# Tokens first, small constants on a second queue, the second block's rows loaded in that block, and dummy products during the load, in a two-block fp32 transformer on one core

## The chip, the cores and the metric

The kernel runs on one NeuronCore of a Trainium2 chip, as one launch. The time is the device time of that core in microseconds (us). The engines in what follows are TensorE (PE, with its weight loads shown apart as PEld), VectorE (DVE), ScalarE (ACT), GpSimd (POOL) and SyncE (SP), which here only issues DMAs. Each engine takes its instructions in a fixed order and waits at semaphores for what another engine or a DMA has not delivered yet.

## The reference, cut to what matters

Two model blocks run one after the other on 256 tokens of width 1024, each with two layers, all in fp32. The part that the change is near is the beginning of each block.

```python
# first block, layer i
u = rmsnorm(h, norm_mix[i])
proj = u @ w_in[i]                                   # gz, ga and gb are among its columns
g = -jnp.exp(a_log) * jax.nn.softplus(ga + dt_bias)  # 8 heads
...
# second block, layer l
u = rms_norm(h, norm1_g[l])
proj = u @ w_in[l]
log_a = log_sigmoid(g_lr @ w_gate2 + b_gate) / 16    # gated linear attention
lam = exp(sum(lq1 * lk1)) - exp(sum(lq2 * lk2)) + lambda_init   # differential attention
```

Between those stand the mixers, a dense and a mixture-of-experts feed-forward part, gated per-layer embeddings, the residual sums and the norms.

## The kernel before

The tokens `h` lie in SBUF as 128 partitions x 2 token halves x 1024. Every large product is done to near fp32 precision out of three reduced-precision products: a weight block `raw` (up to 512 KB) comes by DMA, ACT rounds it into `whi` (line 247), DVE takes the rest into `wlo` (line 248), and PE adds `whi x uh`, `wlo x uh` and `whi x ul` in PSUM (lines 195 to 197, and 221 to 223 for products that come out transposed). `uh` and `ul` are the same two parts of the normed, transposed activations: PE transposes 128x128 pieces of `h` with the identity `ident` (line 263), ACT scales by the norm's weights in `cols` and rounds (line 250), DVE takes the rest (line 251). The norm's factor R comes from squares on ACT (line 281, `junk`) and a Newton iteration on DVE (lines 144 to 152), and is applied after the product.

Weights pass through six `raw` buffers and three pairs of `whi`/`wlo`, so a load waits for the DVE instruction that last read its buffer, and a rounding waits for the PE instruction that last read its pair. SP issues all of the loads.

The order on each engine is set by a scheduler that places instructions by a model of their durations and by priorities. `high_priority(offset=100000)` puts the first loads of `run` ahead of everything. Weight loads have a high priority too, constants have none. A change in the first instructions therefore moves others further on.

`run` begins with the identity, the first half of the tokens' columns, `cols` (161 KB: all norm weights and the convolution's weights of both blocks), the second half of the tokens, and `rows` (400 KB: 800 numbers, read 128 times so that every partition has them). `rows` holds `a_log` and `dt_bias` of the first block (used at line 381, `nea`, and line 376, `xa`) and, for the second block, the four vectors behind `lam` (line 1170, `lt`) and the gate's bias (line 1078, `la`). In the second block the first projections are `grg` and `gla`; 16 columns of `grg` are copied (`glr`, line 1067), transposed on PE (line 1070), copied (`glt`, line 1072) and multiplied by a small weight (line 1076), and `la` adds the bias to that. The next projection, `dq`, runs on PE around these.

Of the kernel before, what the change touches and what calls it, by code (L numbers as in the profile page):

```python
# [9 lines left out]
F32 = mybir.dt.float32  # L10
F32R = mybir.dt.float32r
# [10 lines left out]
RAW2 = 6  # L22
CONV = 800
CRIT = 50
DQ = lambda nc: [nc.scalar]
ORDER = "z v0 v1 v2 v3 rg i0 d0+i1 d1 rq rk rv".split()
D = 1024
# [11 lines left out]
def _consts():  # L39
# [29 lines left out]
    for g, w in enumerate((2, 4, 8, 16)):  # L69
# [16 lines left out]

COLS1 = (("norm_mix", 8), ("norm_ffn", 8), ("norm_ple", 8), ("ret_gn", 8), ("gdn_gn", 1), ("conv_w", 96))
COLS2 = (("norm1_g_2", 8), ("pool_scale_2", 2), ("diff_norm_g_2", 4), ("gla_norm_g_2", 2), ("norm2_g_2", 8), ("norm_final", 8))
ROWS = (("a_log", 8), ("dt_bias", 8), ("diff_lq1_2", 64), ("diff_lk1_2", 64), ("diff_lq2_2", 64),
        ("diff_lk2_2", 64), ("gla_b_gate_2", 128))  # L90


def _offsets(spec):
    o, out = 0, {}
    for l in range(2):
        for n, w in spec:
            out[n, l] = (o, w)
            o += w
    return out, o


COL_AT, NCOL = _offsets(COLS1 + COLS2)
ROW_AT, NROW = _offsets(ROWS)


class Net:
# [27 lines left out]
        return s.cols[:, o:o + w]  # L134

    def row(s, name, l):
        o, w = ROW_AT[name, l]
        return s.rows[:, o:o + w]

    def rsqrt(s, ss, n, mul, add):  # L140

# [1145 lines left out]
    def run(s, out, stop=None):  # L1287
        nc, a = s.nc, s.a
        h = s.hp.tile([P, 2, D], F32, name="h")
        hv = lambda ap: ap.rearrange("(t p) d -> p t d", p=P)  # L1290
        s.cols = s.const.tile([P, NCOL], F32, name="cols")
        with s.tc.high_priority(offset=100000):
            s.ident = s.cst("ident", s.const)
            for c in (0, 512):
                nc.sync.dma_start(h[:, :, c:c + 512], hv(a["x"])[:, :, c:c + 512])
                if c == 0:
                    nc.sync.dma_start(s.cols, a["cols"])
        s.rows = s.const.tile([P, NROW], F32, name="rows")
        src = a["rows"]
        with s.tc.high_priority(offset=100000):  # L1300
            nc.sync.dma_start(s.rows, bass.AP(tensor=src.tensor, offset=src.offset, ap=[[0, P], [1, NROW]]))

        def done(tag):
            if stop == tag:
                nc.sync.dma_start(hv(out), h)
                return True
            return False
        with ExitStack() as es:
            for l in range(2):
                with ExitStack() as e2:  # L1310
                    cp = e2.enter_context(s.tc.tile_pool(name="cp1", bufs=1))
                    s.c = {n: s.cst(n, cp) for n in C1[1:]}
                    s.mixer1(h, l)
                if done(f"mix{l}"):
                    return
                with ExitStack() as e2:
                    yp = e2.enter_context(s.tc.tile_pool(name="yp", bufs=1))
                    y = yp.tile([P, 2, D], F32, name="y")
                    if l == 0:
                        with ExitStack() as e3:  # L1320
                            pp = e3.enter_context(s.tc.tile_pool(name="py", bufs=1))
                            room = [[pp.tile([P, 2, n], F32R, name=f"py{n}{i}") for i in range(2)] for n in (D, T)]
                            run = s.ple_y(y, l, room)
                            u, R = s.norm_t(h, s.col("norm_ffn", l))
                            run()
                        s.swiglu(h, u, R, a["ffn_w_gate"], a["ffn_w_up"], a["ffn_w_down"], 2816)
                        ahead = ()
                    else:
                        pre = yp.tile([P, 2048], F32, name="pre")
                        nc.sync.dma_start(pre.rearrange("p (k c) -> p k c", k=4),  # L1330
                                          a["w_ple_gate"][l][:512, :512].rearrange("(k p) c -> p k c", p=P))
                        ahead = ((0, 2, pre[:, :1024]), (2, 2, pre[:, 1024:]))
                        s.raws.append(e2.enter_context(s.tc.tile_pool(name="raw2", bufs=RAW2)))
                        s.moe(h, l, y)
                    if done(f"ffn{l}"):
                        return
                    s.ple(h, l, y, ahead)
                    s.raws = s.raws[:1]
                if done(f"ple{l}"):
                    return  # L1340
            ur = s.norm_between(h)
        if done("first"):
            return
        with ExitStack() as es:
            cp = es.enter_context(s.tc.tile_pool(name="cp2", bufs=1))
            s.c = {n: s.cst(n, cp) for n in C2}
            s.kz = []
            for i in range(4):
                kz = cp.tile([P, 2, T], F32, name=f"kz{i}")
                nc.gpsimd.memset(kz, 0.0)  # L1350
                s.kz.append(kz)
            for l in range(2):
                s.mixer2(h, l, ur if l == 0 else s.norm_t(h, s.col("norm1_g_2", l)))
                if done(f"mix2{l}"):
                    return
                s.mlp2(h, l)
                if done(f"mlp2{l}"):
                    return
            s.final(h, out, "final_norm_g_2", cp)


def _arrays(inp):

    n = {k: np.asarray(v) for k, v in inp.items()}
    out = {"x": n["x"].reshape(T, D), "pT": n["p"].reshape(2, T, 256).transpose(0, 2, 1)}
    for k in ("w_in", "w_br_ret", "w_br_gdn", "w_out", "w_ple", "w_ple_gate", "w_in_2", "w_out_2", "w_mlp1_2",
              "w_mlp2_2", "pool_w_2", "gla_w_gate2_2", "norm_final", "final_norm_g_2"):
        out[k] = n[k]
    for k in ("ffn_w_gate", "ffn_w_up", "ffn_w_down", "router", "exp_w_gate", "exp_w_up", "exp_w_down"):
        out[k] = n[k][0]  # L1370

    for k in ("w_mlp1_2", "ffn_w_gate", "ffn_w_up"):
        w = out[k].reshape(-1, 8, P, out[k].shape[-1] // P, P).transpose(0, 3, 2, 1, 4)
        out[k] = w.reshape((2,) * (k == "w_mlp1_2") + (-1, P, D))
    cols, rows = [], []
    for l in range(2):
        for k, w in COLS1 + COLS2:
            v = n[k] if k == "norm_final" else n[k][l]
            if k == "conv_w":
                cols.append(v.reshape(4, 24, P).transpose(2, 1, 0).reshape(P, 96))  # L1380
            else:
                cols.append(v.reshape(w, P).T)
        for k, w in ROWS:
            rows.append(n[k][l])
    out["cols"] = np.concatenate(cols, 1)
    out["rows"] = np.concatenate(rows)
    for k, v in _consts().items():
        out["c_" + k] = v
    return {k: np.ascontiguousarray(v) for k, v in out.items()}
# [23 lines left out]
```

## Time and profile before

| | |
|---|---|
| median of 3 runs | 1980.87 us (1978.38 to 1981.93) |
| the profiled execution | 1982.7 us, span of its instructions 1980.8 us |
| PE busy | 1935.2 us, 98% of the span |
| DVE, ACT busy | 1461.8 us (74%), 1187.4 us (60%) |
| mean granted TensorE clock | 0.994 of full speed |
| bytes moved by DMA | 395.47 MB, mean 200 GB/s |

The span is cut by the page into 40 slices, and PE is busy for eight tenths of the first and nine tenths or more of most others. So what any stage is worth is the idle time of PE in it, and whether PE ran at full or at half clock there. Times in rows are counted from the start of the span.

### The profile page before, as it was taken

To read this page: it belongs to the slowest core of one execution; us is meant where nothing else is said; L and a number is where in the kernel's file an instruction comes from. 1 tells how busy PE (TensorE), PEld (TensorE's weight loads), DVE (VectorE), ACT (ScalarE), POOL (GpSimd) and SP (SyncE) were. 2 spreads that over 40 slices of the span, in tenths; PEclk is the share of its full clock that TensorE was granted. 3 is DMA by queue.
4 is the path that set the end of the run, shared out by engine and by line. 5 is a ranking of instruction groups with operands and counts; after the bars stand their busy time and mean duration, and the time that the engine had idled before them with its cause. 6 is when DMAs were issued, how large, how long until landed. Compare 5 with 4: busy or idle time off the path is not lost. (4 is left out here: it accounts for less than half of the span.)

```text
span 1980.8 us, 30212 instructions
## 1 busy us (share of the span) xinstructions
PE 1935.2 (98%) x11194; PEld 1646.6 (83%) x11194; DVE 1461.8 (74%) x2623; ACT 1187.4 (60%) x1889; POOL 13.7 (1%) x29
## 2 busy tenths in 40 slices
PE   8999999999999999999999999998999999999998
PEld 7887787999889877777888888786879898879896
DVE  7987676656479895767998988897877565777565
ACT  7864445544478753446877777776765454565453
POOL 0000000000000000001000000000000000000000
PEclk9999999999999999999999999999999999999999
DMA  8556335555565564356798989994735555525552
GB/s 244 151 172 190 102 134 177 174 184 188 184 184 151 164 187 133 120 192 213 270 347 302 354 297 356 325 353 150 227 107 161 191 190 173 182 97 180 191 182 106
DMA packets 252699, 395.47 MB, mean 200 GB/s; under 512 B 31328, under 2 KB 107264, under 8 KB 252544
## 3 DMA queue, kind: packets, MB, share of 16 engines
q1 hardware_dynamic: 235056, 389.27, 59.9%
q10 hardware_dynamic: 17488, 4.20, 1.1%
q8 instruction: 90, 1.47, 0.3%
q14 instruction: 65, 0.53, 0.1%
HBM read 390.79 MB, written 2.62 MB: 199 GB/s over the span
## 5 line engine op out<-in xcount | busy, mean ns | idle before, releaser
L248 DVE TENSOR_TENSOR wlo<-raw,whi 128x1024 fp32r<-128x1024 f32 (+3 forms) x748 | 878.6, 1184 | 359.3 <-ACT whi L247 349.2
L247 ACT ACTIVATE whi<-raw 128x1024 fp32r<-128x1024 f32 (+3 forms) x748 | 765.5, 1027 | 609.4 <-PE mm L197 362.6
L195 PE MATMUL mm<-whi,uh 128*128 128x512 f32 (+3 forms) x1312 | 505.4, 386 | 4.8 <-ACT mgg L640 2.2
L196 PE MATMUL mm<-wlo,uh 128*128 128x512 f32 (+3 forms) x1312 | 506.9, 387 | 2.3 <-DVE wlo L248 1.9
L197 PE MATMUL mm<-whi,ul 128*128 128x512 f32 (+3 forms) x1312 | 505.7, 387 | 0.3
L196 PEld LDWEIGHTS mm<-wlo,uh 128*128 128x128 f32 x1312 | 248.3, 189 | 55.5 <-DVE wlo L248 9.7
L195 PEld LDWEIGHTS mm<-whi,uh 128*128 128x128 f32 x1312 | 248.0, 189 | 52.4 <-ACT uh L250 3.2
L197 PEld LDWEIGHTS mm<-whi,ul 128*128 128x128 f32 x1312 | 247.8, 189 | 45.9 <-DVE ul L251 1.6
L239 PE MATMUL mm<-uh,whi 128*128 128x256 f32 x864 | 242.6, 281 | 0.8 <-ACT uh L250 0.6
L241 PE MATMUL mm<-uh,wlo 128*128 128x256 f32 x864 | 242.4, 281 | 0.0
L240 PE MATMUL mm<-ul,whi 128*128 128x256 f32 x864 | 242.3, 281 | 0.0
L239 PEld LDWEIGHTS mm<-uh,whi 128*128 128x128 f32 x864 | 162.9, 189 | 1.9 <-ACT uh L250 1.1
L240 PEld LDWEIGHTS mm<-ul,whi 128*128 128x128 f32 x864 | 162.9, 188 | 0.2
L241 PEld LDWEIGHTS mm<-uh,wlo 128*128 128x128 f32 x864 | 162.9, 189 | 0.0
L197 PE MATMUL mm<-whi,hl 128*128 128x512 f32 x344 | 136.4, 397 | 0.0
L196 PE MATMUL mm<-wlo,hh 128*128 128x512 f32 x344 | 135.7, 394 | 0.0
L195 PE MATMUL mm<-whi,hh 128*128 128x512 f32 x344 | 134.5, 391 | 0.0
L223 PE MATMUL mm<-uh,wlo 128*128 128x256 f32 x384 | 109.8, 286 | 0.0
L221 PE MATMUL mm<-uh,whi 128*128 128x256 f32 x384 | 109.6, 285 | 0.0
L222 PE MATMUL mm<-ul,whi 128*128 128x256 f32 x384 | 109.5, 285 | 0.0
L196 PEld LDWEIGHTS mm<-wlo,hh 128*128 128x128 f32 x344 | 64.6, 188 | 15.2
L250 ACT ACTIVATE uh<-pt,cols 128x256 fp32r<-128x256 f32 x152 | 65.0, 472 | 19.6 <-PE pt L263 7.2
(409 smaller groups left out, 2383.6 us busy)
## 6 DMA issues: line engine op xcount, KB each, us to landing
raw<-in_w_in_dram SPq DMA_DIRECT2D x176, 512.0 KB, 3.6
raw<-in_w_mlp_dram SPq DMA_DIRECT2D x128, 512.0 KB, 3.6
raw<-in_exp_w_down_dram SPq DMA_DIRECT2D x80, 512.0 KB, 5.9
raw<-in_exp_w_gate_dram SPq DMA_DIRECT2D x64, 512.0 KB, 5.2
raw<-in_exp_w_up_dram SPq DMA_DIRECT2D x64, 512.0 KB, 5.7
raw<-in_w_out_dram SPq DMA_DIRECT2D x32, 512.0 KB, 3.6
raw<-in_exp_w_gate_dram SPq DMA_DIRECT2D x32, 384.0 KB, 4.4
raw<-in_exp_w_up_dram SPq DMA_DIRECT2D x32, 384.0 KB, 4.0
```

Source lines behind the costliest of these rows:

```text
L195: nc.tensor.matmul(o, uh[:, u0 + k, tk], hi, start=first and k == 0, stop=False)
L196: nc.tensor.matmul(o, uh[:, u0 + k, tk], lo, start=False, stop=False)
L197: nc.tensor.matmul(o, ul[:, u0 + k, tk], hi, start=False, stop=last and k == kt - 1)
L221: nc.tensor.matmul(o[:, m], hi[:, k], uh[:, k, :], start=k == 0, stop=False)
L222: nc.tensor.matmul(o[:, m], hi[:, k], ul[:, k, :], start=False, stop=False)
L223: nc.tensor.matmul(o[:, m], lo[:, k], uh[:, k, :], start=False, stop=k == 7)
L239: nc.tensor.matmul(o[:, i], hi[:, k], uh[:, k, :], start=k == 0, stop=False)
L240: nc.tensor.matmul(o[:, i], hi[:, k], ul[:, k, :], start=False, stop=False)
L241: nc.tensor.matmul(o[:, i], lo[:, k], uh[:, k, :], start=False, stop=k == 7)
L247: nc.scalar.activation(hi, src, AF.Copy)
L248: nc.vector.tensor_sub(lo, src, hi.bitcast(F32))
L250: nc.scalar.activation(hi, src, AF.Copy, scale=col)
```

## The change

Four edits, all around `run`. The tokens are the first loads on SP. The identity, the 8 columns of `cols` that the first norm needs, a shortened `rows` (32 numbers, `a_log` and `dt_bias` of both layers) and the rest of `cols` go through ACT's queue. The other 768 numbers of `rows` become `rows2`, which is loaded by SP in the second block. And DVE clears a 128x512 tile with which PE computes eight products that nobody reads.

```diff
+WARM = 8
-ROWS = (("a_log", 8), ("dt_bias", 8), ("diff_lq1_2", 64), ("diff_lk1_2", 64), ("diff_lq2_2", 64),
-        ("diff_lk2_2", 64), ("gla_b_gate_2", 128))
+ROWS1 = (("a_log", 8), ("dt_bias", 8))
+ROWS2 = (("diff_lq1_2", 64), ("diff_lk1_2", 64), ("diff_lq2_2", 64), ("diff_lk2_2", 64), ("gla_b_gate_2", 128))
...
         s.cols = s.const.tile([P, NCOL], F32, name="cols")
+        s.rows = s.const.tile([P, NROW1], F32, name="rows")
+        src = a["rows"]
+
+        def rows(q, dst, r0):
+            n = dst.shape[-1]
+            q.dma_start(dst, bass.AP(tensor=src.tensor, offset=src.offset + r0, ap=[[0, P], [1, n]]))
+        n0 = COLS1[0][1]
         with s.tc.high_priority(offset=100000):
-            s.ident = s.cst("ident", s.const)
             for c in (0, 512):
                 nc.sync.dma_start(h[:, :, c:c + 512], hv(a["x"])[:, :, c:c + 512])
-                if c == 0:
-                    nc.sync.dma_start(s.cols, a["cols"])
-        s.rows = s.const.tile([P, NROW], F32, name="rows")
-        src = a["rows"]
-        with s.tc.high_priority(offset=100000):
-            nc.sync.dma_start(s.rows, bass.AP(tensor=src.tensor, offset=src.offset, ap=[[0, P], [1, NROW]]))
+            s.ident = s.const.tile([P, P], F32, name="c_ident")
+            nc.scalar.dma_start(s.ident, a["c_ident"])
+            nc.scalar.dma_start(s.cols[:, :n0], a["cols"][:, :n0])
+
+            zero = s.wsp.tile([P, 1024], F32R, name="whi")
+            nc.vector.memset(zero.bitcast(F32)[:, :512], 0.0)
+            idle = s.mm()
+            for _ in range(WARM):
+                nc.tensor.matmul(idle, zero[:, :P], zero[:, :512], start=True, stop=True)
+            rows(nc.scalar, s.rows, 0)
+            nc.scalar.dma_start(s.cols[:, n0:], a["cols"][:, n0:])
...
             s.c = {n: s.cst(n, cp) for n in C2}
+            s.rows2 = cp.tile([P, NROW - NROW1], F32, name="rows2")
+            rows(nc.sync, s.rows2, NROW1)
```

Two rows of Python more stand above the changed part, so line 250 of before is line 252 of after, and so on.

The first place is the beginning of ACT. Before, ACT starts with its function table, `nea` and the squares of the first half of the tokens:

```order
L381 ACT_TABLE_LOAD
L381 ACTIVATE nea_264<-rows_88 128x8
L281 ACTIVATE junk_151,ss_150<-h_81 128x512
L250 ACTIVATE uh_112<-pt_114,cols_82 128x256
L281 ACTIVATE junk_153,ss_150<-h_81 128x512
L250 ACTIVATE uh_112<-pt_114,cols_82 128x256
L250 ACTIVATE uh_112<-pt_123,cols_82 128x256
L247 ACTIVATE whi_192<-raw_190 128x816
```

The same place of ACT in the changed kernel (`whi_204` is the first weight block, as `whi_192` was):

```order
L1305 DMA c_ident_86<-in_c_ident_dram 128x128
L1306 DMA cols_82<-in_cols_dram 128x8
L1299 DMA rows_83<-in_rows_dram 128x32
L1314 DMA cols_82<-in_cols_dram 128x314
L383 ACT_TABLE_LOAD
L383 ACTIVATE nea_276<-rows_83 128x8
L252 ACTIVATE uh_124<-pt_126,cols_82 128x256
L252 ACTIVATE uh_124<-pt_135,cols_82 128x256
L283 ACTIVATE junk_163,ss_162<-h_81 128x512
L252 ACTIVATE uh_124<-pt_126,cols_82 128x256
L249 ACTIVATE whi_204<-raw_202 128x816
```

Four DMA issues stand ahead of the table load. One square stands between the first roundings instead of two, and `nea`, with its wait for `rows`, is still the first computing instruction.

The second place is SP at the beginning of the second block. Before:

```order
L129 DMA c_band_18280<-in_c_band_dram 128x1536
L168 DMA raw_18639<-in_w_in_2_dram 128x2x512
L129 DMA c_bmask_18282<-in_c_bmask_dram 128x256
L129 DMA c_chunk_18284<-in_c_chunk_dram 128x2
L168 DMA raw_18657<-in_w_in_2_dram 128x2x512
L168 DMA raw_18675<-in_w_in_2_dram 128x2x512
L168 DMA raw_18697<-in_w_in_2_dram 128x2x512
L168 DMA raw_18715<-in_w_in_2_dram 128x2x512
L168 DMA raw_18733<-in_w_in_2_dram 128x2x512
L1232 DMA pw_18996<-in_pool_w_2_dram 64x64 x3
L168 DMA raw_18751<-in_w_in_2_dram 128x2x512
```

And in the changed kernel (`raw_18747` is the block that was `raw_18733`):

```order
L131 DMA c_band_18292<-in_c_band_dram 128x1536
L170 DMA raw_18653<-in_w_in_2_dram 128x2x512
L131 DMA c_bmask_18294<-in_c_bmask_dram 128x256
L170 DMA raw_18671<-in_w_in_2_dram 128x2x512
L170 DMA raw_18689<-in_w_in_2_dram 128x2x512
L170 DMA raw_18711<-in_w_in_2_dram 128x2x512
L170 DMA raw_18729<-in_w_in_2_dram 128x2x512
L170 DMA raw_18747<-in_w_in_2_dram 128x2x512
L131 DMA c_chunk_18296<-in_c_chunk_dram 128x2
L1299 DMA rows2_18298<-in_rows_dram 128x768
L170 DMA raw_18765<-in_w_in_2_dram 128x2x512
```

`rows2` stands behind five weight loads, each of which waits for a buffer.

The third place is what uses it, on DVE and on PE. DVE before, around the copies `glr` and `glt`:

```order
L1001 TENSOR_TENSOR R_18270<-R_18270,R_18236 128x2
L248 TENSOR_TENSOR wlo_18642<-raw_18639,whi_18641 128x1024
L1067 COPY glr_18457<-grg_18306 128x2x16
L1072 COPY glt_18463<-pt_18460 128x256
L248 TENSOR_TENSOR wlo_18660<-raw_18657,whi_18659 128x1024
L1078 SCALAR_TENSOR_TENSOR la_18466<-pt_18465,rows_88 128x128 x2
```

DVE in the changed kernel:

```order
L1003 TENSOR_TENSOR R_18282<-R_18282,R_18248 128x2
L250 TENSOR_TENSOR wlo_18674<-raw_18671,whi_18673 128x1024
L1069 COPY glr_18471<-grg_18320 128x2x16
L1172 TENSOR_TENSOR lt_18785<-rows2_18298 128x64 x2
L1173 TENSOR_REDUCE ls_18786<-lt_18785 128x2
L1074 COPY glt_18477<-pt_18474 128x256
L1080 SCALAR_TENSOR_TENSOR la_18480<-pt_18479,rows2_18298 128x128 x2
```

PE before, from the first product of `dq` (`mm_18619` and `mm_18620`) to the small weight's product with `glt`:

```order
L195 MATMUL mm_18619<-whi_18623,uh_18172 128x512
L196 MATMUL mm_18619<-wlo_18624,uh_18172 128x512
L1070 MATMUL pt_18460<-c_ident_83,glr_18457 128x128 x2
L197 MATMUL mm_18619<-whi_18623,ul_18173 128x512
L195 MATMUL mm_18620<-whi_18623,uh_18172 128x512
L196 MATMUL mm_18620<-wlo_18624,uh_18172 128x512
L1076 MATMUL pt_18465<-w2_18454,glt_18463 128x128
```

PE in the changed kernel, the last part of the same stretch, in front of which stand nine more products of `dq`:

```order
L197 MATMUL mm_18634<-whi_18637,uh_18184 128x512
L198 MATMUL mm_18634<-wlo_18638,uh_18184 128x512
L1072 MATMUL pt_18474<-c_ident_86,glr_18471 128x128 x2
L199 MATMUL mm_18634<-whi_18637,ul_18185 128x512
L197 MATMUL mm_18633<-whi_18655,uh_18184 128x512
L198 MATMUL mm_18633<-wlo_18656,uh_18184 128x512
L1078 MATMUL pt_18479<-w2_18468,glt_18477 128x128
```

The products with `rows2` (`lt`) now stand on DVE ahead of `glt`, which PE's last row waits for; PE comes to that row nine products of `dq` later than before (14 of them stand ahead of it, where there were 5).

## Rows read from the trace of the kernel before

**Rows 1.** The page, busy time of each engine over the whole span.
```profile
PE 1935.2 (98%) x11194; PEld 1646.6 (83%) x11194; DVE 1461.8 (74%) x2623; ACT 1187.4 (60%) x1889; POOL 13.7 (1%) x29
```
**Rows 2.** Waits of PE: line, what released it: us in total, times, longest.
```profile
PE pt L263 <- DMA h<-in_x_dram: 7.7, 1, 7.7
...
PE pt L701 <- ACT qkt L699: 4.1, 2, 2.1
...
PE pt L516 <- ACT cs L411: 2.0, 2, 1.4
...
PE pt L392 <- DVE g L384: 1.1, 2, 0.9
```
**Rows 3.** Timeline of SP, 0 to 8 us: start, us, engine, line, what.
```profile
1.20 0.42 SPq L1301 DMA_DIRECT2D rows<-in_rows_dram  x1
1.66 0.43 SPq L1295 DMA_DIRECT2D h<-in_x_dram  x1
...
3.12 6.62 SPq L168 DMA_DIRECT2D raw<-in_w_in_dram  x5
```
**Rows 4.** DMA issues, 0 to 40 us: count, KB each, median us to landing.
```profile
h<-in_x_dram SPq DMA_DIRECT2D x2, 512.0 KB, 6.3
raw<-in_w_in_dram SPq DMA_DIRECT2D x2, 408.0 KB, 7.7
rows<-in_rows_dram SPq DMA_DIRECT2D x1, 400.0 KB, 4.6
```
**Rows 5.** Timeline of ACT, 0 to 13 us.
```profile
5.85 0.21 ACT L381 ACTIVATE nea<-rows 128x8 f32<-128x8 f32 x1 [3.84 <-DMA rows<-in_rows_dram]
...
8.77 0.47 ACT L250 ACTIVATE uh<-pt,cols 128x256 fp32r<-128x256 f32 x1 [0.51 <-PE pt L263]
...
10.84 0.88 ACT L247 ACTIVATE whi<-raw 128x816 fp32r<-128x816 f32 x1
```
**Rows 6.** Timeline of PE, 7 to 13.4 us.
```profile
7.65 3.69 PE L263 MATMUL pt<-c_ident,h 128*128 128x128 f32 x16 [7.65 <-DMA h<-in_x_dram]
11.77 0.51 PE L195 MATMUL mm<-whi,uh 128*128 128x272 f32 x2 [0.42 <-ACT whi L247]
12.81 0.39 PE L196 MATMUL mm<-wlo,uh 128*128 128x272 f32 x1 [0.53 <-DVE wlo L248]
13.04 0.29 PE L197 MATMUL mm<-whi,ul 128*128 128x272 f32 x1
13.17 0.29 PE L196 MATMUL mm<-wlo,uh 128*128 128x272 f32 x1
```
**Rows 7.** Groups of POOL's instructions by line and form: busy, mean ns.
```profile
L1350 POOL MEMSET kz<- 128x512 f32 x4 | 1.9, 532 | 0.0
```
**Rows 8.** PE after the longest wait on `qkt`: window 248 to 255 us, timeline within.
```profile
248.00:255.00 7.00, 7.00 (x23) 5.57 (x24) 1.60 (x4) 2.46 (x4) 0.00 (x0) 0.61 0.38 142
...
250.02 0.63 PE L197 MATMUL mm<-whi,ul 128*128 128x512 f32 x1
250.45 0.63 PE L195 MATMUL mm<-whi,uh 128*128 128x512 f32 x1
```
**Rows 9.** DMA issues in the second block, 1400 to 1420 us, as in Rows 4.
```profile
raw<-in_w_in_dram SPq DMA_DIRECT2D x5, 512.0 KB, 3.6
...
gb<-in_final_norm_g_dram SPq DMA_DIRECT2D x1, 512.0 KB, 5.8
```
**Rows 10.** Timeline of SP, 1408 to 1408.8 us.
```profile
1408.36 0.37 SPq L168 DMA_DIRECT2D raw<-in_w_in_dram  x1
```
**Rows 11.** Timeline of DVE, 1385 to 1432 us.
```profile
1395.45 0.35 DVE L1170 TENSOR_TENSOR lt<-rows 128x64 f32<-128x64 f32 x2
1395.84 0.29 DVE L1171 TENSOR_REDUCE ls<-lt 128x2 f32<-128x128 f32 x1
...
1412.16 0.42 DVE L1072 COPY glt<-pt 128x256 f32<-128x256 f32 x1 [0.55 <-PE pt L1070]
```
**Rows 12.** Timeline of PE, 1404 to 1432 us.
```profile
1412.67 0.45 PE L1076 MATMUL pt<-w,glt 128*128 128x128 f32 x2
```

More of the change, by code (lines that the diff above doesn't have):

```diff
@@ L88, with _offsets @@
 COLS2 = (("norm1_g_2", 8), ("pool_scale_2", 2), ("diff_norm_g_2", 4), ("gla_norm_g_2", 2), ("norm2_g_2", 8), ("norm_final", 8))
-ROWS = (("a_log", 8), ("dt_bias", 8), ("diff_lq1_2", 64), ("diff_lk1_2", 64), ("diff_lq2_2", 64),
-        ("diff_lk2_2", 64), ("gla_b_gate_2", 128))
-def _offsets(spec):
-    o, out = 0, {}
+ROWS1 = (("a_log", 8), ("dt_bias", 8))
+ROWS2 = (("diff_lq1_2", 64), ("diff_lk1_2", 64), ("diff_lq2_2", 64), ("diff_lk2_2", 64), ("gla_b_gate_2", 128))
+def _offsets(spec, o=0):
+    out = {}
     for l in range(2):
@@ L102 @@
 COL_AT, NCOL = _offsets(COLS1 + COLS2)
-ROW_AT, NROW = _offsets(ROWS)
+ROW_AT, NROW1 = _offsets(ROWS1)
+ROW2_AT, NROW = _offsets(ROWS2, NROW1)
 class Net:
@@ L136, in row @@
     def row(s, name, l):
-        o, w = ROW_AT[name, l]
-        return s.rows[:, o:o + w]
+        o, w = (ROW_AT if (name, l) in ROW_AT else ROW2_AT)[name, l]
+        return s.rows[:, o:o + w] if o < NROW1 else s.rows2[:, o - NROW1:o - NROW1 + w]
     def rsqrt(s, ss, n, mul, add):
@@ L1382, in _arrays @@
                 cols.append(v.reshape(w, P).T)
-        for k, w in ROWS:
-            rows.append(n[k][l])
+    for spec in (ROWS1, ROWS2):
+        rows += [n[k][l] for l in range(2) for k, w in spec]
     out["cols"] = np.concatenate(cols, 1)
```

## The prediction

> **What bounds the kernel.** I read the page's busy row first: PE works 1935.2 us of 1980.8 [rows 1], so only about 46 us of the span are free of it, and an edit off PE is worth what it takes out of those, or out of stretches at half clock. Then the waits of PE, longest first [rows 2]: 7.7 us at the very beginning, for the tokens; 4.1 for `qkt` in two waits; 2.0 for `cs` (longest 1.4) and 1.1 for `g` (longest 0.9). The first is what the change is about. Then the beginning by engine, to see what ends last there: SP's issues [rows 3] with their time to landing [rows 4], ACT's first rows [rows 5] and PE's [rows 6]. The reader is to see a relay. SP issues the tokens behind the identity and the 400 KB `rows`; the first half lands at about 7.6, and PE transposes it. ACT rounds the first piece at 8.77 and the first weight block at 10.84, which is just when that block lands (issued 3.12, 7.7 to landing). PE's first real product starts at 11.77, waits for `wlo`, and from 12.81 on PE hardly stops. So after the tokens it is the first weight block and ACT's queue that set the start, and a gain at the tokens need not arrive whole.
>
> **The clock at the start.** Two products of 272 columns start 0.23 us apart at 12.81 and 13.04, the next 0.13 apart [rows 6]: PE ran at 1.2 GHz until about 13.0 and at 2.4 GHz after it. The transposes and the first three products were slow. But little of that is on the path: from 8.77 to 11.77 PE waits for ACT.
>
> **Part A, the beginning.** SP's first issue is one spacing of 0.46 before the row at 1.20 [rows 3], at 0.74. That slot goes to the tokens. With nothing ahead of them they land between 3.6 us later (the quickest loads of the same 512 KB [rows 9]), at 4.3, and 6.3 later (their own median [rows 4]), at 7.0. I take 4.6, near the former, since what stood ahead has gone and the identity is 64 KB. The dummies: clearing 128x512 is not shown on DVE; on POOL it takes 0.53 [rows 7]. From 0.7, that is 1.25. Eight products of 512 columns start 0.43 apart at half clock [rows 8], 3.4 in all, so they end at 4.7, and the transposes start at 4.8 instead of 7.65. The dummies then hide behind the load, and if the tokens land at 4.3 they cost 0.4. The first rounding follows 1.1 later, as before (7.65 to 8.77), at 5.9: 2.9 earlier.
>
> Two waits could come up at that point. ACT's first computing instruction is still `nea`, which waits for `rows`; that is now 16 KB, issued third on ACT at about 1.7, and even with the 4.6 of the old load it is there at 6.3, 0.4 to 0.6 late. And DVE's first computing instruction still waits for the last part of `cols`. I count both as hidden by the tokens' transposes and keep 0.6 for the bound.
>
> The first weight block is issued after two token loads, at 1.7 instead of 3.12, with 400 KB less ahead of it. It lands between 6.5 and 7.7 later, at 8.2 to 9.4; I take 8.2. Its rounding takes 0.88 [rows 5], so PE's first product is at 9.1 instead of 11.77, 2.65 earlier. Of that, ACT's new order takes some back. Before the fourth block's rounding stand both squares and two pieces of the second token half; that rounding waits for the first pair of `whi`/`wlo`, which PE gives back 16 products of 0.13 after its start at 10.15, at 12.3; and two more pieces of the tokens stand behind it. PE then has no piece five for some 0.8 us. That leaves 1.8. I take 0.3 off for a start at half clock (second rival) and count A as -1.5, with 0 and -2.9 as its ends: nothing, if `rows` or the first block is late, and all of the first rounding's lead.
>
> **Part B, the order.** From the first projections to the end of the first mixer (some 250 us) the scheduler places instructions of PE, ACT and DVE in another order; from there to the second block the order is as before. The trace does not show the new one. The work is the same, and PE's waits in that stretch outside `qkt` are mostly one of 1.4 for `cs` and one of 0.9 for `g` [rows 2]. They could both go, or come twice: -2.3 to +2.3. I take 0, since nothing in the rows favours a sign. The wait for `qkt` stays: its rounding is still behind a weight rounding that waits for PE's last product before it.
>
> **Part C, `rows2`.** It is issued behind the weight load of 1408.36 [rows 10], 0.37 long, and behind `c_chunk` with an issue of about 0.43 [rows 3]: at 1409.2. It is 384 KB, read 128 times over like `rows` (4.6 to landing) and `gb` (512 KB, 5.8 [rows 9]), with one 512 KB block ahead in the queue. Its ends are 3.6 (a weight block [rows 9]), 1412.8, and 7.7 (the first weight block [rows 4]), 1416.9. I take 5.2, between `rows` and `gb`: 1414.4. DVE waits there with `lt`, and behind it in its queue stand `glt`, `la`, the softplus chain and the roundings of the next blocks. `lt`, its sum and `glt` take 0.35 + 0.29 + 0.42 [rows 11], so `glt` is ready at 1415.5. Before, PE came to its product with `glt` at 1412.67 [rows 12]; now it does nine products of `dq` first, 9 x 0.22 at full clock (half of 0.43), and comes at 1414.7. PE waits 0.8. The bounds are 0 (all hidden by `dq`) and 1416.9 + 1.1 - 1414.7 = 3.3. The roundings behind cost nothing as long as the three pairs hold: DVE is up to three pairs of 12 products ahead, some 2.6 us of PE each.
>
> **Sum.** -1.5 + 0 + 0.8 = -0.7. Against the profiled execution's own 1982.7 that is 1982.0. That execution stood 1.8 above the median of the runs, 1980.87, so in terms of the median I forecast 1980.2.
>
> **A rule against the change.** Between its last dummy-warmed transpose (about 6.6) and its first product at 9.1, PE is idle again. The trace shows what can follow: after the longest of the waits on `qkt` (2.1), the window from 248 to 255 has PE busy all 7 us at a granted clock of 0.61, with products of 512 columns 0.43 apart [rows 2, 8]. The Trainium skill says in "TensorE: Matmul & The Clock Gate", Part 1, that an array which has been idle goes back to 1.2 GHz, and its part on why this matters asks for no long gap between bursts. By that rule the dummies warm PE for nothing; the trace agrees with the fall, and the second rival is its price.
>
> **Rivals.**
> 1. The beginning's lead arrives whole. A is -2.9, the new order loses both waits of B (-2.3), and `rows2` lands in time: -5.2, 1975.7. For it: PE has nothing but the tokens to wait for until 7.65, and `dq` covers a landing of 4.4 us. Against it: the first weight block and ACT's queue stand between. Chance 0.20.
> 2. The warm-up is lost, so that the change does not do what it says. The first products run at half clock: 18 products of the first block at 0.23 instead of 0.13 are 1.8, which is what A gave. A is 0, C stays: +0.8, 1981.7. For it: the fall after `qkt`. Against it: PE may wait elsewhere then anyway. Chance 0.12.
> 3. Slower: `rows2` stops DVE and PE in the second block. It lands 7.7 after its issue, PE waits 3.3 at its product with `glt`, and the wait halves the clock as after `qkt`, 7 us x 0.39 = 2.7: with A, -1.5 + 3.3 + 2.7 = +4.5, 1985.4. It decides from a landing of about 1417 on. For it: DVE and PE both stand in order behind one load that is issued late, behind weight blocks. Against it: `rows` itself took 4.6. Chance 0.10.
>
> My forecast keeps 0.58, with a range of its own from 1977.9 to 1982.6.
>
> **How the numbers follow.** The limits of faster and slower lie at 0.2%, 4.0 us, about what a measurement can tell here (the runs of before reach over 3.6 us): below 1976.9 and above 1984.8. Faster: most of rival 1 (0.17) and 0.03 of the forecast's low end, 0.20. Slower: 0.08 of rival 3, 0.02 of the forecast and 0.01 of rival 2, 0.11. The same: 0.69. The range goes to 1976.2 below, through the middle of rival 1, and to 1984.4 above, short of rival 3, which leaves out about 0.2.
>
> **What would show it.** A: in the changed profile the first transposes start near 4.8, the first product near 9.1, and the wait for the tokens shrinks from 7.7 to under 1, with eight dummies before it. If that product comes after 10.5, the block's landing or `nea` was mis-sized. The clock: products of 272 columns 0.13 apart from the first on, or 0.23. B: the waits for `cs` and `g`, gone or repeated. C: at line 1078 of the changed kernel a wait of PE for DVE of 0 to 1.5, and at line 1172 one of DVE for `rows2`. A time below 1976 or above 1985 would mean that a term is wrong and not only a size.

## The result and the profile after

The changed kernel takes 1997.05 us in the median of 6 runs (1994.24 to 1999.85), the kernel before 1981.82 on the same chip (1978.38 to 1983.36). The ratio is 1.0079 with a 95% interval of 1.0069 to 1.0089: slower by 15 us, where 1980.2 was forecast. The profiled execution took 1999.85, with a span of 1998.1 and a mean granted clock of 0.986 (0.994 before).

The page's busy row [rows 1] has become:

```profile
PE 1950.3 (98%) x11202; PEld 1658.3 (83%) x11202; DVE 1460.8 (73%) x2624; ACT 1186.0 (59%) x1888; POOL 13.7 (1%) x29
```

PE computes the same and eight dummies more, but is busy for 15 us longer: 3.8 of them are the dummies, and most of the rest is work that ran at half clock. The waits of PE in after, columns as in [rows 2]:

```profile
PE mm L197 <- ACT whi L249: 4.5, 2, 3.9
...
PE pt L703 <- ACT qkt L701: 3.7, 2, 2.1
PE pt L551 <- DVE Tn L541: 3.2, 2, 2.4
...
PE pt L1224 <- DVE sc L1217: 1.9, 1, 1.9
...
PE pt L551 <- ACT X L552: 1.5, 1, 1.5
```

The 7.7 for the tokens is gone, `qkt` is as it was, and the largest that are new or longer stand in three places: one at the beginning (`whi`), one inside the first mixer (`Tn`, `X`), one in the second block (`sc`).

Where the time went is read by pairing each PE instruction of before with the same one of after (same line, same tiles, same number of its kind) and taking the median difference of their starts in bins of 20 us. This lag is worked out, not a row of a view:

```
us of before    20   140   220   640   900   1340   1400   1520   1940
lag of after  +1.7  -0.4  +7.7  +7.7  +8.1  +10.8  +11.8  +17.4  +17.3
```

So 8.1 us come in one step between 140 and 220, 5.7 between 1400 and 1520, and 4.1 in small steps between. The beginning is worse at first (+1.7) and made good by 140.

**The beginning.** Timeline of after, rows of ACT, of DVE and of PE (columns as in [rows 5]):

```profile
8.04 0.21 ACT L383 ACTIVATE nea<-rows 128x8 f32<-128x8 f32 x1 [3.96 <-DMA rows<-in_rows_dram]
...
9.45 0.17 DVE L997 TENSOR_TENSOR gg<-cols 128x8 f32<-128x8 f32 x1 [8.05 <-DMA cols<-in_cols_dram]
...
1.46 3.78 PE L1312 MATMUL mm<-whi 128*128 128x512 f32 x8 [1.46 <-DVE whi L1309]
5.04 2.46 PE L265 MATMUL pt<-c_ident,h 128*128 128x128 f32 x16
11.35 0.82 PE L197 MATMUL mm<-whi,uh 128*128 128x272 f32 x2 [3.85 <-ACT whi L249]
12.79 0.43 PE L199 MATMUL mm<-whi,ul 128*128 128x272 f32 x1
13.02 0.43 PE L198 MATMUL mm<-wlo,uh 128*128 128x272 f32 x1
```

Tokens, dummies and transposes come as forecast (transposes at 5.04 instead of 7.65, at full clock). Then `nea` holds ACT until 8.04 for 16 KB, and `gg`, DVE's first computing instruction, holds DVE until 9.45 for the rest of `cols`. The first product starts at 11.35, only 0.4 earlier than in [rows 6], and the products behind it are 0.23 apart, at half clock, until 16.4.

**The first mixer.** At 190 us PE begins the triangular inverse of the gated delta rule. Its input comes back from DRAM: DVE computes small inverses, ACT issues four writes (`dt`) and four reads (`tc`), DVE copies them to `Tn`, PE takes `Tn` (line 549 of before, 551 of after) and ACT copies the product to `X`. Timeline of the kernel before, rows of ACT, of DVE and of PE:

```profile
176.92 0.65 ACTq L498 DMA_DIRECT2D dt<-X  x1
...
186.04 1.75 ACTq L501 DMA_DIRECT2D tc<-dt  x4
...
189.82 0.28 DVE L539 COPY Tn<-tc 32x256 f32<-32x256 f32 x1 [2.86 <-DMA tc<-dt]
...
190.16 0.69 PE L549 MATMUL pt<-Tn,A 32*32 32x32 f32 x16 [0.51 <-DVE Tn L539]
194.78 0.69 PE L549 MATMUL pt<-Tn,A 32*32 32x32 f32 x16
```

The same rows in the timeline of the changed kernel, with the roundings of ACT around `X`:

```profile
178.31 0.65 ACTq L500 DMA_DIRECT2D dt<-X  x1
...
187.54 3.46 ACTq L503 DMA_DIRECT2D tc<-dt  x4
...
197.63 1.06 ACT L249 ACTIVATE whi<-raw 128x1024 fp32r<-128x1024 f32 x1 [4.53 <-PE mm L199]
198.71 0.37 ACT L552 ACTIVATE X<-pt 32x256 f32<-32x256 f32 x1
...
193.23 0.28 DVE L541 COPY Tn<-tc 32x256 f32<-32x256 f32 x1 [4.78 <-DMA tc<-dt]
...
193.57 0.86 PE L551 MATMUL pt<-Tn,A 32*32 32x32 f32 x16 [2.44 <-DVE Tn L541]
...
196.24 0.63 PE L197 MATMUL mm<-whi,uh 128*128 128x512 f32 x1
196.66 0.63 PE L198 MATMUL mm<-wlo,uh 128*128 128x512 f32 x1
199.14 0.69 PE L551 MATMUL pt<-Tn,A 32*32 32x32 f32 x16 [1.54 <-ACT X L552]
```

Two things stand in another order. On ACT, one weight rounding more comes ahead of the `dt` writes (55 from the start instead of 54), and it waits for PE; so the reads are issued 1.5 later. And on PE, 7 and 5 large products stand between the first three steps of the inverse, where 14 and 10 stood; the other 12 now come before it.

PE waits 2.44 for `Tn` instead of 0.51. The late issue alone does not explain that, since PE comes to the step later too: 3.6 after the first read's issue in both kernels (189.65 and 191.13, the start of the step less its wait). What grew is the way back: from that issue to the copy `Tn` it is 3.8 in before and 5.7 in after. DMA issues of before, 174 to 200 us (columns as in [rows 4]):

```profile
tc<-dt ACTq DMA_DIRECT2D x4, 128.0 KB, 4.7
```

Of after, the same stretch:

```profile
tc<-dt ACTq DMA_DIRECT2D x4, 128.0 KB, 6.3
```

Seven products later PE waits 1.54 for `X`, and here the order does explain it: on ACT `X` is behind a rounding that waited 4.53 for PE, so it cannot come before those products are done. In before, 14 products covered the same rounding and copy, and PE did not wait. From 194.96 on, the products of 512 columns are 0.43 apart: half clock. Two windows of the kernel before (window, length, busy time and count of PE, PEld, DVE, ACT and POOL, granted clock, DMA share, GB/s):

```profile
180.00:220.00 40.00, 38.28 (x339) 29.77 (x338) 20.02 (x29) 16.25 (x29) 0.46 (x1) 1.00 0.54 149
200.00:220.00 20.00, 20.00 (x212) 16.63 (x212) 9.50 (x17) 6.57 (x16) 0.46 (x1) 1.00 0.31 97
```

The same windows of after:

```profile
180.00:220.00 40.00, 35.57 (x219) 27.38 (x218) 15.08 (x21) 11.91 (x16) 0.46 (x1) 0.79 0.50 129
200.00:220.00 20.00, 19.82 (x134) 15.61 (x135) 8.20 (x13) 5.65 (x9) 0.46 (x1) 0.66 0.29 98
```

From 200 to 220 PE is busy nearly all the time in both, and gets through 134 instructions instead of 212. From 180 to 220 it is busy for 35.57 us instead of 38.28. So of the 8.1 us some 2.7 are more waiting, and the rest, about 5, is work at half clock.

**The second block.** Timeline of after, rows of DVE and of PE:

```profile
1425.92 0.36 DVE L1172 TENSOR_TENSOR lt<-rows 128x64 f32<-128x64 f32 x2
...
1488.59 1.23 DVE L250 TENSOR_TENSOR wlo<-raw,whi 128x1024 fp32r<-128x1024 f32 x1
1489.73 0.35 DVE L1217 SCALAR_TENSOR_TENSOR sc<-sc,mx 128x128 f32<-128x128 f32 x1
...
1427.36 0.47 PE L1078 MATMUL pt<-w,glt 128*128 128x128 f32 x2
...
1490.22 0.30 PE L1224 MATMUL pt<-c_ident,sc 128*128 128x128 f32 x1 [1.94 <-DVE sc L1217]
```

`lt` shows no wait for `rows2`, and PE none at line 1078. But 60 us later, in the differential attention, `sc` stands behind a `wlo` of 1.23 on DVE, and PE waits 1.94 for it. That wait is a third of the 5.7. Between 1395 and 1530 PE waits 4.4 in all, 1.0 in before; another 0.9 is for `grg`, the first projection's copy on ACT. The rest, some 2, goes with the granted clock, which is 0.91 from 1480 to 1500 and was 1.00.

### The profile page after: what moved, and what is told of

Read it like the earlier page. It is cut to its first block, busy times and chain, and to the rows that moved or that the text cites. A ratio compares the mean times of both kernels' runs of the same rounds, so it can differ in the third digit from the quotient of the medians.

```text
span 1998.1 us, 30227 instructions
## 1 busy us (share of the span) xinstructions
PE 1950.3 (98%) x11202; PEld 1658.3 (83%) x11202; DVE 1460.8 (73%) x2624; ACT 1186.0 (59%) x1888; POOL 13.7 (1%) x29
## 5 line engine op out<-in xcount | busy, mean ns | idle before, releaser
L253 DVE SCALAR_TENSOR_TENSOR ul<-pt,cols,uh 128x256 fp32r<-128x256 f32 x152 | 67.2, 478 | 16.1 <-ACT uh L252 15.4
```

The costliest lines, as they stand in the source:

```text
L253: nc.vector.scalar_tensor_tensor(lo, src, col, hi.bitcast(F32), op0=OP.mult, op1=OP.subtract)
```

## The experiments

The theory: the four edits cost little themselves; the loss comes because they make the scheduler place instructions differently in two stretches of which the edits do not speak. The rival: the loads, their queue or the dummies cost directly. Each kernel ran beside the kernel before on the same chip, and each "beside" below is that kernel's median there. "Inverse" is the lag gained between 140 and 220 us, "block 2" that between 1400 and 1520, both in the one profiled execution; "clock" is the mean granted clock from 190 to 220.

| kernel | ratio to before, 95% | order at the inverse | inverse | clock | block 2 |
|---|---|---|---|---|---|
| changed | 1.0079 (1.0069 to 1.0089) | changed | +8.1 | 0.72 | +5.7 |
| e1 | 1.0080 (1.0067 to 1.0092) | changed | +7.4 | 0.72 | +6.6 |
| e2 | 1.0027 (1.0017 to 1.0037) | before | +1.4 | 1.00 | +5.7 |
| e3 | 1.0051 (1.0038 to 1.0065) | changed | +8.0 | 0.72 | -0.3 |
| e4 | 1.0003 (0.9994 to 1.0012) | before | +0.9 | 1.00 | -0.3 |
| e5 | 1.0052 (1.0039 to 1.0065) | changed | +6.5 | 0.77 | -0.3 |
| e6 | 1.0070 (1.0057 to 1.0083) | a third | +7.5 | 0.89 | +5.9 |
| e7 | 1.0000 (0.9989 to 1.0011) | before | +0.1 | 1.00 | -0.3 |
| e8 | 1.0020 (1.0008 to 1.0032) | before | +3.2 | 0.94 | -0.3 |
| e9 | 1.0073 (1.0058 to 1.0089) | changed to the second step, then before | +4.0 | 0.89 | +4.3 |
| e10 | 0.9997 (0.9989 to 1.0006) | before | +4.9 | 0.89 | 0.0 |
| e11 | 1.0008 (0.9998 to 1.0017) | before | +2.0 | 1.00 | -0.3 |
| e12 | 1.0013 (1.0002 to 1.0024) | before | +1.1 | 1.00 | -0.3 |

The lags of single executions overlap: e10, in the order of before, lost 4.9 in its profiled one (it waits 1.08 for `Tn` and 1.84 for `wlo` there, and the clock falls), and e9 only 4.0. The medians do not: with the second block in the order of before, the changed order of the inverse stands at 1.0051 and 1.0052, and the order of before between 0.9997 and 1.0020.

Two things go through all of these profiles. In every kernel but e6 PE comes to the inverse 3.5 to 3.7 after the first read's issue, so that its wait for `Tn` is set by how late this read is back: 3.5 to 4.9 from issue to landing in the order of before, 4.5 to 5.7 in the changed one (e9 with it). And the wait for `X` is 1.54 to 1.56 in the four kernels of the changed order, and in none of the others.

### e1: no dummies

```diff
-            zero = s.wsp.tile([P, 1024], F32R, name="whi")
-            nc.vector.memset(zero.bitcast(F32)[:, :512], 0.0)
-            idle = s.mm()
-            for _ in range(WARM):
-                nc.tensor.matmul(idle, zero[:, :P], zero[:, :512], start=True, stop=True)
```


> The changed kernel without the clearing on VectorE and without the eight dummy products; every engine's order is otherwise the changed kernel's, row for row. Theory 1 (the new order of the first mixer and of the second block's first mixer is what costs): the loss stays, 1995 to 2000; the first transposes run at half clock, about 1 later than in the changed kernel, hidden by the wait of nea. Theory 2 (the dummies cost: they take weight buffers or wear out the clock early): back to 1985 or less.

Measured 1999.13 beside 1983.88. The dummies neither cost nor bring anything here: PE transposes at half clock (3.65 instead of 2.46) and still comes to its first product at 11.30, since ACT and DVE hold it.

### e2: two issues on ScalarE's queue swapped

```diff
+            nc.scalar.dma_start(s.cols[:, n0:], a["cols"][:, n0:])
             rows(nc.scalar, s.rows, 0)
-            nc.scalar.dma_start(s.cols[:, n0:], a["cols"][:, n0:])
```


> The changed kernel with its last two issues on ScalarE's queue swapped, so that the long rest of cols is issued before the short rows. By the order of instructions, TensorE then has the order of the kernel before from its 20th row to the end of the first block, and the changed kernel's order in the second block. Theory 1 (order): the 8 us lost between 180 and 220 do not come, 1988 to 1991; nea waits up to 1 us longer at the start. Rival (the loads themselves, their queue or their place in memory cost): 1996 to 1999, as the changed kernel.

Measured 1988.65 beside 1983.88: 10 us come back by one swap. At the inverse PE waits 0.92 for `Tn`, 1.18 for a `wlo` and not at all for `X`, at full clock. The start is better too, because the scheduler now puts `nea` behind the roundings. Timeline of e2, rows of ACT and of PE:

```profile
4.74 0.63 ACT L283 ACTIVATE junk<-h 128x512 f32<-128x512 f32 x1 [0.66 <-DMA h<-in_x_dram]
...
8.59 0.88 ACT L249 ACTIVATE whi<-raw 128x816 fp32r<-128x816 f32 x1 [1.00 <-DMA raw<-in_w_in_dram]
...
9.53 0.77 PE L197 MATMUL mm<-whi,uh 128*128 128x272 f32 x2 [2.01 <-ACT whi L249]
```

The lag at 20 us is -1.1 (it was +1.7), at 220 it is -1.1 (+7.7). Of the difference of 8.8 at 220, some 2 stand at 140 already and are the start's; the rest is the inverse's.

### e3: rows2 loaded at the start

```diff
+        s.rows2 = s.const.tile([P, NROW - NROW1], F32, name="rows2")
...
             rows(nc.scalar, s.rows, 0)
             nc.scalar.dma_start(s.cols[:, n0:], a["cols"][:, n0:])
+            rows(nc.scalar, s.rows2, NROW1)
...
-            s.rows2 = cp.tile([P, NROW - NROW1], F32, name="rows2")
-            rows(nc.sync, s.rows2, NROW1)
```


> The changed kernel with rows2 loaded at the start, as the last issue on ScalarE's queue, and not in the second block. The order is the changed kernel's in the first block and the kernel before's in the second. Theory 1 (order): the 5 us lost between 1420 and 1500 do not come, 1991 to 1993. Rival (that loss is the clock's or the buffers', and would come in any order): 1996 to 1999. If the late rows2 itself made the wait, as the prediction's third rival has it, 1 to 3 less than the changed kernel.

Measured 1993.76 beside 1983.88. The second block's loss is gone, the first mixer's is whole.

### e4: both

The edits of e2 and e3 together:

```diff
+            nc.scalar.dma_start(s.cols[:, n0:], a["cols"][:, n0:])
             rows(nc.scalar, s.rows, 0)
-            nc.scalar.dma_start(s.cols[:, n0:], a["cols"][:, n0:])
+            rows(nc.scalar, s.rows2, NROW1)
...
-            rows(nc.sync, s.rows2, NROW1)
```


> Both: the two issues swapped and rows2 loaded at the start as the last on ScalarE's queue. From the 20th instruction on, TensorE, VectorE and ScalarE have the order of the kernel before in the whole program; tokens first, second queue and dummies stay. Theory 1 (order): 1981 to 1985, which is the kernel before plus what the start costs or gives (-0.4 to +2). Rival (the loads): 1992 or more.

Measured 1983.63 beside 1983.88. The two losses add up: e4 is at before, e2 and e3 stand 0.27% and 0.51% above it, the changed kernel 0.79%. Tokens first, the second queue and the dummies are all still there, so together they cost nothing that can be measured, and bring nothing; the dummies were also tried apart (e1, e7).

### e5: tokens first, nothing else

On the kernel before:

```diff
...
-            s.ident = s.cst("ident", s.const)
             for c in (0, 512):
                 nc.sync.dma_start(h[:, :, c:c + 512], hv(a["x"])[:, :, c:c + 512])
                 if c == 0:
-                    nc.sync.dma_start(s.cols, a["cols"])
+                    s.ident = s.cst("ident", s.const)
...
+            nc.sync.dma_start(s.cols, a["cols"])
             nc.sync.dma_start(s.rows, bass.AP(tensor=src.tensor, offset=src.offset, ap=[[0, P], [1, NROW]]))
```


> The kernel before with one edit: on SyncE the first half of the tokens is issued first, then the identity, the second half, cols and rows. No second queue, no dummies, rows not split. By the order of instructions the first mixer then has, from the triangular inverse of the first four heads on, TensorE's order of the changed kernel, and the second block that of the kernel before. Theory 1 (order): although the loads are nearly those of before, TensorE waits and loses clock between 180 and 220 as in the changed kernel, 5 to 9 above the kernel before. Rival (queue, dummies or split rows cost, the order is harmless): within 2 of the kernel before.

Measured 1993.75 beside 1983.41. One edit out of four makes the first mixer's loss, with PE's waits of 1.34 and 1.55 at the inverse and a clock of 0.66 from 200 to 220. TensorE and ScalarE have the changed kernel's order there; VectorE's agrees with neither kernel throughout. That and e2 speak from both sides: the loss goes with the order, not with queue, dummies or split rows.

### e6: half of the writes issued by GpSimd

```diff
-                    q[0].dma_start(dt.rearrange("(r e) b m i c -> e i (b m) r c", e=2)[e, 1], tt[at])
+                    nc.gpsimd.dma_start(dt.rearrange("(r e) b m i c -> e i (b m) r c", e=2)[e, 1], tt[at])
```


> The changed kernel in which the two writes of tt into dt, in both layers of the first block, are issued by GpSimd instead of ScalarE. ScalarE then issues two writes in a row instead of four, and TensorE has 20 and 10 products between the first steps of the inverse where it had 7 and 5. Theory 1 (TensorE waits because the round trip through DRAM is issued late on ScalarE, and has few products to cover it): the waits at the inverse's first step, 3.9 in two, shrink under 1, the half clock after them does not come, and the lag at 200 us falls from 7.7 to under 2: 1990 to 1994. Rival (the transfers themselves are slow beside the weight loads): the waits stay over 3, 1996 to 2000.

Measured 1995.34 beside 1983.41: a miss; the rival's sign, waits of over 3, came. PE has 20 and 10 products between the steps now and no wait for `X`, but comes to the inverse at 188.4 (191.1 in after), 1.6 after the first read's issue, and `Tn` comes at 192.28 (193.23): it waits 4.19 once, and at another place 4.8 for `qkt`. The half clock only comes earlier: 0.59 from 195 to 200, full from 200 to 220. The first read is issued at 186.83, 0.7 earlier than in after, and lands 5.4 later; so it is the reads that are slow here, as in after.

### e7: e4 without dummies

On e4:

```diff
-            zero = s.wsp.tile([P, 1024], F32R, name="whi")
-            nc.vector.memset(zero.bitcast(F32)[:, :512], 0.0)
-            idle = s.mm()
-            for _ in range(WARM):
-                nc.tensor.matmul(idle, zero[:, :P], zero[:, :512], start=True, stop=True)
```


> The kernel with the two issues swapped and rows2 loaded at the start, without the clearing and the dummies, the order otherwise the same. Here the wait of nea is gone, so the dummies could show. If the transposes are not on the path (the first weight block lands later than they end): within 1 of that kernel, which stood at the kernel before. If the prediction's part A was right that transposes at full clock bring the start forward: 1 to 2 slower than with the dummies.

Measured 1983.92 beside 1983.41, as e4. Transposes at half clock end at 8.5, the first product starts at 9.73 (9.69 with dummies): it waits for the first weight block.

### e8: twelve dummies behind the transposes

```diff
             u, R = s.norm_t(h, s.col("norm_mix", l))
+            if l == 0:
+                idle = s.mm()
+                for _ in range(12):
+                    nc.tensor.matmul(idle[:, :256], u[0][:, 2, :P], u[0][:, 2, :256], start=True, stop=True)
```


> The kernel with the two issues swapped and rows2 loaded at the start, and besides the eight dummies twelve more of 256 columns, between the transposes and the first weight block's products, on data that is there by then; the order otherwise the same. If the idle time between the transposes and the first product is what drops the clock (the prediction's second rival): the products of 272 columns start 0.13 apart at once instead of 0.23, and the start gains 1 to 2. Rival (the clock falls whatever stands there, or the dummies delay the products by as much): no gain, or a loss up to 1.

On e4. Measured 1987.39 beside 1983.41, 1.0020. The dummies end at 8.95, the first product starts at 10.48 (1.53 of wait for its rounding), and the products are 0.23 apart until 14.6. Idle time was left, so the run decides nothing about the clock.

### e9: X copied by VectorE

```diff
-                    nc.scalar.activation(X2[r, :, :32], eight(px[r]), AF.Copy)
+                    nc.vector.tensor_copy(X2[r, :, :32], eight(px[r]))
```


> The changed kernel in which VectorE instead of ScalarE makes the first copy of the triangular inverse, X from PSUM (line 552), in both layers of the first block. Loads and the stretch before the inverse stay as they are. In the changed kernel that copy stood on ScalarE behind a weight rounding that waited for TensorE. Theory 1, in detail: of the two waits at the inverse's first step the second (1.5, for X) goes, the first (1.2 to 2.4, for Tn) stays; the lag at 200 us is 1.5 lower, and if the half clock between 200 and 220 hangs on both waits together, up to 4 more: 1991 to 1996. Rival (X is not what TensorE waits for, the copy comes later on VectorE as well): a wait of over 1 stays at that place, 1996 to 2000.

On the changed kernel. Measured 1996.43 beside 1983.64. In the profile the wait for `X` is gone (PE waits 0.73 for `uh` on ACT behind the second step), that for `Tn` is 2.12, and the clock is 0.56 from 195 to 200 and 0.94 from 200 to 220. But the edit moved more than the copy: from the second step of the inverse on PE has the order of before, with 10 products ahead of the third step instead of 5. And the profiled execution was the fastest of six (1992.25), and the intervals of this kernel and the changed one overlap. So the run agrees with the trace on why the second wait comes, but does not give its worth.

### e10: e4 with qkt copied by VectorE

```diff
-                nc.scalar.activation(qkt, p, AF.Copy)
+                nc.vector.tensor_copy(qkt, p)
```


> The kernel with the two issues swapped and rows2 loaded at the start, in which VectorE instead of ScalarE copies qkt (line 701) in both layers. The order to the end of the inverse is that of the kernel before. If a copy on ScalarE behind a weight rounding that waits for TensorE is the pattern that costs, TensorE's waits for qkt (4.1 in two) go, and with them half clock after 247: 4 to 7 faster than the kernel before, 1976 to 1980. Rival (the copy waits as long on VectorE, or the wait for mgg takes its place): within 2 of the kernel before.

Measured 1982.82 beside 1983.64: the rival. PE no longer waits for `qkt`; it waits 3.15 for the next copy on ACT instead. Timeline of e10, row of PE:

```profile
249.92 0.79 PE L197 MATMUL mm<-whi,uh 128*128 128x512 f32 x1 [3.15 <-ACT mgg L642]
```

### e11: rows2 loaded between the mixers

```diff
-            rows(nc.scalar, s.rows2, NROW1)
...
                 if done(f"mix{l}"):
                     return
+                if l == 0:
+                    rows(nc.sync, s.rows2, NROW1)
```


> The changed kernel with the two last issues swapped, and with rows2 issued by SyncE after the first layer's mixer, so neither at the start nor in the second block. From the 20th instruction on the order is the kernel before's in both blocks. If the start forecast by the prediction's part A is right once nothing waits for nea (-1.5), and rows2 costs nothing between: 1 to 2 faster than the kernel before. If the start's lead is given back later, as in the kernel with rows2 at the start: within 1.

On e4. Measured 1983.42 beside 1981.52, 1.0008: no gain. The start gains 2.0 by 20 us, the forecast's size; by 1940 the lag is +1.3. The lead is given back in small steps, the largest of them, 2.0, at the inverse, where PE waits 1.57 for a `wlo`.

### e12: sixteen dummies behind the transposes

On e11:

```diff
+            if l == 0:
+                idle = s.mm()
+                for _ in range(16):
+                    nc.tensor.matmul(idle[:, :256], u[0][:, 2, :P], u[0][:, 2, :256], start=True, stop=True)
```


> The same with sixteen dummy products of 256 columns between the transposes and the first weight block's products, in the order of the kernel before otherwise. With rows2 out of the way the first block lands earlier, so the dummies should reach it. If the idle time before the first product drops the clock: products of 272 columns 0.13 apart from the first on, and 1 to 2 faster than the same kernel without them. Rival: they start 0.23 apart all the same; no gain.

Measured 1983.73 beside 1981.52, 1.0013. Timeline of e12, rows of PE:

```profile
10.39 0.52 PE L197 MATMUL mm<-whi,uh 128*128 128x272 f32 x2 [0.88 <-ACT whi L249]
...
11.66 0.28 PE L199 MATMUL mm<-whi,ul 128*128 128x272 f32 x1
11.78 0.29 PE L198 MATMUL mm<-wlo,uh 128*128 128x272 f32 x1
```

The same of e11:

```profile
9.65 0.52 PE L197 MATMUL mm<-whi,uh 128*128 128x272 f32 x2 [2.44 <-ACT whi L249]
10.93 0.29 PE L199 MATMUL mm<-whi,ul 128*128 128x272 f32 x1
11.06 0.29 PE L198 MATMUL mm<-wlo,uh 128*128 128x272 f32 x1
```

And of e2:

```profile
10.96 0.43 PE L199 MATMUL mm<-whi,ul 128*128 128x272 f32 x1
11.19 0.43 PE L198 MATMUL mm<-wlo,uh 128*128 128x272 f32 x1
```

With the sixteen dummies the products run at full clock, but so they do in e11, which has none of them, and in e2, with the same loads up to there, they don't. No gain: the start is 0.7 later.

No version beat the kernel before.

## Why the prediction was wrong, step by step

**Part B failed, and with it the forecast.** It counted the new order of the first mixer at 0 with ends of 2.3, "since nothing in the rows favours a sign", and built the ends from two waits that were there, for `cs` and `g`; it passed over others in the same stretch (1.1 for `mgg`, 0.8 for `wlo`, 0.5 for `Tn`). The order makes +8.1 (e2, e5: it goes and comes with the order, although the loads are nearly the same). Of the forecast's terms, A was -1.5 and the lag by 140 us is -0.4, B was 0 and is +8.1, C was 0.8 and is +5.7.

The row to read was not a large wait but a small one: 0.51 for `Tn` at 190.16, at the end of a chain over DRAM that DVE itself waited 2.86 for. It says that the chain has no slack: whatever the first read takes beyond 3.6 is waiting. And a count of products shows the second wait: `X` stands behind a rounding that needs PE's products of the same stretch, and with 7 of them instead of 14 PE is done before ACT is. The prediction counted neither. And the price was taken as the wait alone, while the half clock behind it cost more than the waits did.

**Part C was right in what it worked out and wrong in what it left out.** `rows2` was issued at 1420.6; less the lag of 12 that is 1408.6, and 1409.2 was forecast. It took 4.7 to land (5.2 assumed), DVE's `lt` and PE's line 1078 waited for nothing (0.8 forecast, 0 to 3.3). But the order of the block changed with it, and the largest wait came 60 us later at `sc`: +5.7 with the wait for `grg` and the clock, gone in all eight kernels that load these numbers elsewhere. Rival 3, the slower one, named the right edit and sign, and a mechanism that did not occur.

**Part A: the loads were right, the two waits were not hidden.** The tokens were there at 5.0 (e1, with no dummies ahead, transposes from 4.97; 4.6 forecast), and the transposes began at 5.04 (4.8). "I count both as hidden" is the step that failed: `rows` took 6.3 us for 16 KB, not 4.6, and `cols` 7.2; `nea` then let ACT begin at 8.04, so that the first product was at 11.35 instead of 9.1. Where `nea` stands later, it is at 9.5 to 9.7 (e2, e4, e7, e11) and the start gains 1.1 (e2) and 2.0 (e11), beside the 1.5 forecast, but only 0.5 in e4 and e7, which also load `rows2` there.

**Rival 2, the clock at the start, came true and did not matter.** The products were 0.23 apart until 16.4. The Trainium skill ("TensorE: Matmul & The Clock Gate", Part 1) has the array fall back when it has been idle, and says that the same kernel meets the change at another point from run to run. The runs are in line with both: after falls behind its 3.85 of idle time, and e11, idle for 2.44 before its first product where e2, with the same order there, is for 2.01, does not fall where e2 does.

**The rest,** 4.1 us between 220 and 1400, comes after 700 us, where the order is the same in both kernels. Single profiles cannot tell it from chance: it is -0.7 to +7.2 in the other kernels, and medians of kernels with the old order (e4, e7) agree with before to 0.1%. What is left open: how much of the 8.1 would stay if PE waited as long but kept its clock (e9 changed more than that), and why the first read of the round trip through DRAM takes 3.5 us to land in one run (e4) and 5.7 in another (after), with two weight loads under way beside it in both; that the order does this is not shown. That the order of before be forced under exactly the changed loads was not tried: e2 moves one issue, and `nea` with it.

## What to carry to other kernels

Where a scheduler sets the order, an edit at the start is an edit of every stretch that it reorders: compare the two orders stretch by stretch, and weigh each by the chains that have no slack left, which show as small waits at the end of long round trips. Look also for a copy that stands behind an instruction which itself waits for the engine that needs the copy. A swap of two small loads can then be worth more than the whole change, in either direction, so before an edit is judged, try it with a neighbour that gives the old order back. An instruction that needs a small late load must not stand first on an engine that others wait for.

## What the runs showed of the hardware that was not expected

The same stall does not always cost the same clock. From 920 to 960 PE waits for the same two things (1.1 and 0.8) in before, after and e12, in the same order and with the same busy time, and gets another clock each time. A window of before (columns as above):

```profile
920.00:960.00 40.00, 38.15 (x233) 33.05 (x232) 29.58 (x83) 31.20 (x55) 5.55 (x4) 1.00 0.43 136
```

Of after:

```profile
920.00:960.00 40.00, 38.14 (x214) 32.98 (x214) 26.07 (x75) 26.55 (x48) 5.54 (x4) 0.91 0.50 170
```

Of e12:

```profile
920.00:960.00 40.00, 38.13 (x218) 32.93 (x217) 30.03 (x85) 30.00 (x52) 5.55 (x4) 0.96 0.36 112
```

After loses 2.6 us of lag there for no other reason that the profile shows. Such places may be why runs of the kernel before alone reach from 1979.39 to 1988.21.

On the second queue small loads were not quick beside the tokens and the first weights: 16 KB took 6.3 us to landing and 4 KB 4.9, while each 512 KB half of the tokens took 4.4 on the first queue. DMA issues of after, 0 to 14 us (columns as in [rows 4]):

```profile
h<-in_x_dram SPq DMA_DIRECT2D x2, 512.0 KB, 4.4
...
cols<-in_cols_dram ACTq DMA_DIRECT2D x1, 157.0 KB, 7.2
...
cols<-in_cols_dram ACTq DMA_DIRECT2D x1, 4.0 KB, 4.9
rows<-in_rows_dram ACTq DMA_DIRECT2D x1, 16.0 KB, 6.3
```
